# Low half of a weight chunk: one VectorE subtract over 1024 columns in place of two over 512

## The chip, the cores and the metric

One core of a Trainium2 chip. The metric is the device time of one execution in microseconds (us); a change counts by the median of its runs beside runs of the kernel before on the same chip.

## The reference, cut to what matters

The program is a chain of two models on 256 tokens of width 1024: a two-layer block (gated feed-forward, a mixer, feed-forward again, a gated per-layer embedding), then a two-layer block with modulation, pooling, attention and a squared-ReLU feed-forward of width 4096. Nearly all its arithmetic is matrix products with float32 weights.

```python
def swiglu(x, w_in, w_out):
    gate, up = jnp.split(x @ w_in, 2, axis=-1)
    return (jax.nn.silu(gate) * up) @ w_out

def first_block(x, ...):                       # two layers
    h = h + 0.5 * rmsnorm(swiglu(rmsnorm(h, g[0]), ffn1_w_in[i], ffn1_w_out[i]), g[1])
    h = h + rmsnorm(mix, g[3])                  # even_mixer, then odd_mixer
    h = h + 0.5 * rmsnorm(swiglu(rmsnorm(h, g[4]), ffn2_w_in[i], ffn2_w_out[i]), g[5])
    h = h + rmsnorm(jax.nn.sigmoid(h @ ple_w_gate[i]) * (p[i] @ ple_w_proj[i]), g[6])

def second_block(x, c, ctx, ...):              # two layers, latent and context tokens
    h_lat = h_lat + g1[:, None, :] * y_l        # pool_mix, then attn_mix
    h_lat = h_lat + g2[:, None, :] * sq_relu_mlp(m_l, mlp_w1[i], mlp_w2[i])
    return rms_norm(h_lat, final_g)
```

## The kernel before, in words

Weights stream from HBM once, in chunks of 128 partitions by 1024 float32 columns (512 KB). `split` (L221 to L236) takes in one chunk: a DMA on SP's queue (L227) fills a tile `raw`, ScalarE (ACT) rounds it into the high part `wh` (L232), and VectorE (DVE) makes the low part `wl` as `raw - wh` (L235), in two instructions over 512 columns each. `mm3` (L238 to L241) then makes each product out of three matmuls: high times high, and the two products of a high and a low part. Depending on the stage, the weight is the matmul's moving operand (512 columns at a time, `tok_group`, `out_multi`) or its stationary one (128 columns at a time, `feat_tile`, which goes through the eight 128-column blocks of a chunk in order).

Buffers: four `raw` tiles (`NRAW`), seven pairs of `wh` and `wl` (`NR`), so a chunk can be split up to seven chunks ahead of its matmuls. `raw` comes free when both ACT and DVE have read it. A few chunks go through tiles of their own: `rawx`, `whx`, `wlx` at the end of a feed-forward block, `rawf`, `whf`, `wlf` for the context tokens. In all there are 534 chunks.

DVE has other work: the small steps of the junctions between stages (`xTl` L336, `yt` L362, `h` L367, `ta`, `aro`, `mmx`, the low parts of activations L245 and L250), and side work that makes modulation vectors (`jka` L974, 1024 columns each). GpSimd (POOL) makes the reciprocal roots of the norms: DVE writes a mean square (`ms`, L272 or L296), POOL raises it to the power -0.5 (`rs`, L274 or L298), DVE goes on with the product by it (`mxn` L1010 and L1092, `axn` L1315, `h` L367). The tile framework plans the order of the instructions of each engine at build time, by priorities that follow the program's order and by when an instruction can start in its plan; each engine then runs its list in that order. In that plan the two halves of a chunk are two instructions, and other DVE work may stand between them.

Of the kernel before, what the change touches and what calls it, by code (L numbers as in the profile page):

```python
# [9 lines left out]
F32 = mybir.dt.float32  # L10
# [4 lines left out]
ALU = mybir.AluOpType  # L15
# [154 lines left out]
def tile_model(ctx: ExitStack, tc: tile.TileContext, A, out):  # L170
    nc = tc.nc
    V, S, G, T, Y = nc.vector, nc.scalar, nc.gpsimd, nc.tensor, nc.sync
# [24 lines left out]
    for t in range(2):  # L197
        for n in range(2):
            sl = slice(512 * n, 512 * n + 512)
# [21 lines left out]
    def split(r, chunk, i, wp=None):  # L221
        wpool, wt, wb = wp or (r.w, r.tag, None)
        if wp:
            src = wpool.tile([128, 1024], F32, name="raw" + wt, tag="raw" + wt, bufs=RXB)
        else:
            src = r.raw.tile([128, 1024], F32, name="raw" + r.tag, tag="raw" + r.tag)
        Y.dma_start(src, chunk[:, 1024 * i:1024 * i + 1024])  # L227
        wh = wpool.tile([128, 1024], F32R, name="wh" + wt, tag="wh" + wt, bufs=wb)
        wl = wpool.tile([128, 1024], F32R, name="wl" + wt, tag="wl" + wt, bufs=wb)
        cnt[0] += 1  # L230
        with after(fed[0]) if KEEP < cnt[0] <= KEEP + LATE and r is M else nullcontext():
            S.activation(wh, src, AF.Copy)  # L232
            for q in range(2):
                sl = slice(512 * q, 512 * q + 512)
                V.tensor_tensor(wl[:, sl], src[:, sl], wh[:, sl].bitcast(F32), op=ALU.subtract)  # L235
        return wh, wl  # L236

    def mm3(o, a, b, first, last):  # L238
# [109 lines left out]
    def after(ins):  # L348
        return tc.issue_after(ins) if ins is not None else nullcontext()
# [80 lines left out]
    def out_multi(items, acc, first, last, step=None, extra=0, pool=None, tail=False):  # L430
        ws = []
        for q, (c, hid, k0) in enumerate(items):
            wp = (pool, "x", 2 * extra) if q < extra else None
            ws += [(split(M, c, i, wp), hid, k0 + i) for i in range(2)]
        m = len(ws)
        for t in range(2):
            js = [j for j in range(m)]
            if t and tail:
                order = [(sl, j) for sl in TAIL for j in js]
            elif t:  # L440
                js = js[2 * extra:] + js[:2 * extra]
                order = [(n, j) for j in js for n in range(2)]
            else:
                order = [(n, j) for n in range(2) for j in js[:-2]] + [(n, j) for n in range(2) for j in js[-2:]]
            for n, j in order:
                w, hid, k = ws[j]
                sl = n if isinstance(n, slice) else slice(512 * n, 512 * n + 512)
                mm3(acc[t][:, sl], xk(hid, k, t), (w[0][:, sl], w[1][:, sl]), first and j == 0,
                    last and j == js[-1])
            if step is not None:  # L450
                step(t)
# [6 lines left out]
    def ffn(x, win, wout, np_, pool, hooks, joint):  # L458
# [16 lines left out]
        def inp(i):  # L475
            hid = xt_tiles(2, pool, "hid", 4)
            for j in range(2):
                ps = bank(name="fin")
                for u in range(2):
                    feat_tile(ps[:, 256 * u:256 * u + 256], split(M, win[2 * i + j], u), x.xt)  # L480
                s = pool.tile([128, 256], F32, name="sil", tag="sil", bufs=2)
                V.tensor_tensor(s, ps[:, 0:256], rb, op=ALU.mult)
                S.activation(s, s, AF.Silu)
                V.tensor_tensor(s, s, ps[:, 256:512], op=ALU.mult)
                hilo(hid[0][:, j, :], hid[1][:, j, :], s)
            return hid
# [46 lines left out]
    def group512(chunks, xt, skew=False, name="g5"):  # L533
        ps = pacc.tile([128, 1024], F32, name=name, tag="acc")
        ps = ps.rearrange("p (t n) -> p t n", t=2)
        if skew:
            ws = [split(M, c, u) for c in chunks for u in range(2)]
            tok_group(ps, xt, ws, 0, 8, 512, True, True)
        else:
            for i in range(2):  # L540
                tok_group(ps, xt, [split(M, chunks[i], u) for u in range(2)], 4 * i, 4, 512, i == 0, i == 1)
        return ps
# [1070 lines left out]
```

## Time and profile before

| | us |
|---|---|
| median of 3 runs | 1932.61 (1931.67 to 1932.79) |
| span of the profiled execution | 1926.2 |
| busy: PE matmul | 1856.4 |
| busy: DVE | 1338.0 |
| busy: ACT | 925.8 |
| busy: POOL | 56.8 |

The span goes from the first instruction to the last of one profiled execution; the time of a run holds what lies around it too. The profiled execution's own time outside the span is not shown; between its span and the median lie 6.4 us. Busy time of an engine is the time in which at least one of its instructions ran. Matmuls overlap, so PE's busy time says where PE had nothing to do, not how near it is to its peak.

### The profile page before, as it was taken

What the parts mean: (1) busy time and instruction counts of PE and PEld (TensorE: products, weight loads), DVE (VectorE), ACT (ScalarE), POOL (GpSimd) and SP (SyncE); (2) the same over time, 40 slices, a digit from 0 to 9 for tenths busy, and PEclk for the clock granted to TensorE, in tenths of its full rate; (3) what the DMA queues carried; (4) which work ended last, traced back from release to release, by engine and by line L of the source; (5) the groups of instructions that cost most, each with busy time, mean ns of one, the idle gap of its engine ahead of it and who ended that gap; (6) DMA issues with size and microseconds to landing.
All of it is one profiled execution on the core that took longest, in us unless ns stands there. A gap on an engine that the chain in (4) does not pass through costs nothing.

```text
span 1926.2 us, 29706 instructions
## 1 busy us (share of the span) xinstructions
PE 1856.4 (96%) x11425; PEld 1636.7 (85%) x11425; DVE 1338.0 (69%) x2531; ACT 925.8 (48%) x1452; POOL 56.8 (3%) x95
## 2 busy tenths in 40 slices
PE   7999999999989999999999998899999999999998
PEld 6999777899969998888789997798999987667997
DVE  6997666999679976765587867854444468656555
ACT  6544657544474445444454455632323335544443
POOL 0000000000000000000000000100000002000000
PEclk9999999999999999999999999999999999999999
DMA  8886534887568865655488857333232324216552
GB/s 274 286 272 223 173 104 144 278 276 256 161 213 269 276 217 192 230 164 166 159 280 306 300 191 255 130 112 99 88 101 98 98 67 134 88 61 196 191 186 78
DMA packets 100950, 356.06 MB, mean 185 GB/s; under 512 B 12249, under 2 KB 13129, under 8 KB 100809
## 3 DMA queue, kind: packets, MB, share of 16 engines
q1 hardware_dynamic: 100088, 353.30, 55.2%
q8 instruction: 89, 1.46, 0.3%
q10 hardware_dynamic: 720, 0.88, 0.1%
q14 instruction: 53, 0.43, 0.1%
HBM read 353.03 MB, written 1.10 MB: 184 GB/s over the span
## 4 chain that ended last, share of the span: by engine, by line
PE 75%; issue 11%; DVE 6%; ACT 3%; DMA 3%; POOL 2%; SPq 0%; POOLq 0%; ACTq 0%; DVEq 0%
PE finm L239 8%; PE finm L241 8%; PE finm L240 8%; PE acc L239 8%; PE acc L241 7%; PE acc L240 7%; PE g L241 2%; PE g L239 2%; PE g L240 2%; PE mfinm L239 2%; PE mfinm L241 2%; PE mfinm L240 2%; DVE wlm L235 2%; PE cfof L239 2%; PE cfof L241 1%
## 5 line engine op out<-in xcount | busy, mean ns | idle before, releaser
L235 DVE TENSOR_TENSOR wlm<-rawm,whm 128x512 fp32r<-128x512 f32 x1048 | 683.8, 686 | 340.3 <-ACT whm L232 337.3
L232 ACT ACTIVATE whm<-rawm 128x1024 fp32r<-128x1024 f32 x524 | 550.1, 1058 | 560.0 <-PE finm L240 154.8
L239 PE MATMUL finm<-xTh,whm 128*128 128x256 f32 x1280 | 362.6, 283 | 0.0
L240 PE MATMUL finm<-xTl,whm 128*128 128x256 f32 x1280 | 362.5, 283 | 0.0
L241 PE MATMUL finm<-xTh,wlm 128*128 128x256 f32 x1280 | 362.5, 283 | 0.0
L240 PEld LDWEIGHTS finm<-xTl,whm 128*128 128x128 f32 x1280 | 243.7, 190 | 1.7
L239 PEld LDWEIGHTS finm<-xTh,whm 128*128 128x128 f32 x1280 | 243.8, 190 | 1.6
L241 PEld LDWEIGHTS finm<-xTh,wlm 128*128 128x128 f32 x1280 | 243.6, 190 | 0.0
L239 PE MATMUL acc<-whm,hidh 128*128 128x512 f32 x544 | 215.6, 397 | 1.9 <-ACT hidh L244 1.9
L241 PE MATMUL acc<-whm,hidl 128*128 128x512 f32 x544 | 214.8, 395 | 0.0
L240 PE MATMUL acc<-wlm,hidh 128*128 128x512 f32 x544 | 214.4, 395 | 0.0
L974 DVE SCALAR_TENSOR_TENSOR jka<-rawa,sv 128x1024 bf16<-128x1024 f32 x160 | 195.2, 1220 | 27.2 <-DMA rawa<-in_adw_dram 26.4
L239 PE MATMUL g<-whm,xTh 128*128 128x512 f32 x320 | 129.4, 404 | 10.1 <-ACT xTh L335 3.4
L241 PE MATMUL mfinm<-xTh,wlm 128*128 128x256 f32 x480 | 135.7, 283 | 0.0
L240 PE MATMUL mfinm<-xTl,whm 128*128 128x256 f32 x480 | 135.5, 282 | 0.0
L239 PE MATMUL mfinm<-xTh,whm 128*128 128x256 f32 x480 | 135.4, 283 | 0.0
L241 PE MATMUL g<-whm,xTl 128*128 128x512 f32 x320 | 129.2, 404 | 0.5 <-DVE xTl L250 0.4
L240 PE MATMUL g<-wlm,xTh 128*128 128x512 f32 x320 | 127.6, 399 | 0.0
L239 PEld LDWEIGHTS acc<-whm,hidh 128*128 128x128 f32 x544 | 103.4, 190 | 23.6 <-ACT hidh L244 3.4
L241 PEld LDWEIGHTS acc<-whm,hidl 128*128 128x128 f32 x544 | 102.8, 189 | 22.2 <-DVE hidl L245 0.5
L240 PEld LDWEIGHTS acc<-wlm,hidh 128*128 128x128 f32 x544 | 103.0, 189 | 21.3 <-DVE wlm L235 0.2
L239 PEld LDWEIGHTS mfinm<-xTh,whm 128*128 128x128 f32 x480 | 91.4, 190 | 0.7
(465 smaller groups left out, 3130.0 us busy)
## 6 DMA issues: line engine op xcount, KB each, us to landing
rawm<-in_m_dram SPq DMA_DIRECT2D x128, 512.0 KB, 3.7
rawa<-in_adw_dram SPq DMA_DIRECT2D x96, 512.0 KB, 5.5
rawm<-in_f1i_dram SPq DMA_DIRECT2D x88, 512.0 KB, 5.1
rawm<-in_f2i_dram SPq DMA_DIRECT2D x88, 512.0 KB, 4.9
rawm<-in_odi_dram SPq DMA_DIRECT2D x48, 512.0 KB, 4.3
rawm<-in_f1o_dram SPq DMA_DIRECT2D x40, 512.0 KB, 5.8
rawm<-in_f2o_dram SPq DMA_DIRECT2D x40, 512.0 KB, 5.3
rawm<-in_evi_dram SPq DMA_DIRECT2D x22, 512.0 KB, 4.0
```

Of the source, the lines that this page charges most:

```text
L232: S.activation(wh, src, AF.Copy)
L235: V.tensor_tensor(wl[:, sl], src[:, sl], wh[:, sl].bitcast(F32), op=ALU.subtract)
L239: T.matmul(o, a[0], b[0], start=first, stop=False)
L240: T.matmul(o, a[0], b[1], start=False, stop=False)
L241: T.matmul(o, a[1], b[0], start=False, stop=last)
L974: V.scalar_tensor_tensor(jk, src, 1.0, sv[v], op0=ALU.mult, op1=ALU.mult, accum_out=adacol[:, l, v, 2 * i + f:2 * i + f + 1])
```

## The change

The loop over two halves goes; one instruction computes all 1024 columns of `wl`. Nothing else is changed: the same data, tiles, DMAs and matmuls.

```diff
         with after(fed[0]) if KEEP < cnt[0] <= KEEP + LATE and r is M else nullcontext():
             S.activation(wh, src, AF.Copy)
-            for q in range(2):
-                sl = slice(512 * q, 512 * q + 512)
-                V.tensor_tensor(wl[:, sl], src[:, sl], wh[:, sl].bitcast(F32), op=ALU.subtract)
+            V.tensor_tensor(wl, src, wh.bitcast(F32), op=ALU.subtract)
         return wh, wl
```

## Rows read from the trace of the kernel before

**Rows 1.** The page: span, busy time and instructions of each engine.
```profile
span 1926.2 us, 29706 instructions
PE 1856.4 (96%) x11425; PEld 1636.7 (85%) x11425; DVE 1338.0 (69%) x2531; ACT 925.8 (48%) x1452; POOL 56.8 (3%) x95
```
**Rows 2.** Busy time by stretch: length, PE, PEld, DVE, ACT, POOL, granted clock, DMA.
```profile
320.00:352.00 32.00, 26.63 (x120) 20.03 (x120) 25.48 (x55) 24.44 (x46) 3.99 (x8) 0.95 0.71 244
352.00:545.00 193.00, 192.97 (x1305) 178.48 (x1304) 159.60 (x291) 91.50 (x123) 1.12 (x2) 1.00 0.69 233
...
1155.00:1245.00 90.00, 77.58 (x458) 66.30 (x457) 73.68 (x146) 54.01 (x106) 8.58 (x13) 0.94 0.58 198
1245.00:1560.00 315.00, 315.00 (x2077) 287.06 (x2076) 145.54 (x228) 95.55 (x120) 0.00 (x0) 1.00 0.31 99
1560.00:1745.00 185.00, 171.26 (x776) 130.54 (x774) 128.75 (x300) 91.63 (x210) 16.77 (x14) 1.00 0.29 94
```
**Rows 3.** Waits over the span: who waited for whom, us, times, longest.
```profile
DVE wlm L235 <- ACT whm L232: 337.3, 198, 8.2
...
ACT whm L232 <- PE finm L240: 154.8, 102, 4.0
```
**Rows 4.** Lines L235 and L890: instructions of each kind, ns min/median/max, first and last.
```profile
L235 DVE TENSOR_TENSOR wlm<-rawm,whm x1048: 671/685/695, 9.7 to 1899.5; 128x512 fp32r<-128x512 f32 x175
...
L235 DVE TENSOR_TENSOR wlx<-rawx,whx x16: 670/684/686, 51.7 to 977.5; 128x512 fp32r<-128x512 f32 x16
...
L890 DVE TENSOR_TENSOR y<-y,ronb x4: 1217/1226/1227, 793.3 to 910.4; 128x1024 f32<-128x1024 f32 x4
```
**Rows 5.** DVE's timeline at two places: start us, us, what.
```profile
66.23 1.29 DVE L235 TENSOR_TENSOR wlm<-rawm,whm 128x512 fp32r<-128x512 f32 x2
67.44 1.22 DVE L974 SCALAR_TENSOR_TENSOR jka<-rawa,sv 128x1024 bf16<-128x1024 f32 x1
...
793.27 1.22 DVE L890 TENSOR_TENSOR y<-y,ronb 128x1024 f32<-128x1024 f32 x1
794.41 0.41 DVE L897 TENSOR_TENSOR oam<-oattm,decay 128x256 f32<-128x256 f32 x1
```
**Rows 6.** The chain by line: whole span, then 1155 to 1245, 1605 to 1660 us.
```profile
PE finm L239 8%; PE finm L241 8%; PE finm L240 8%; PE acc L239 8%; PE acc L241 7%; PE acc L240 7%; PE g L241 2%; PE g L239 2%; PE g L240 2%; PE mfinm L239 2%; PE mfinm L241 2%; PE mfinm L240 2%; DVE wlm L235 2%; PE cfof L239 2%; PE cfof L241 1%
...
by line: DMA prow<-rows 10.6%; DMA rawf<-in_plw_dram 8.0%; DVE wlm L235 6.7%; issue 5.7%; PE pptf L1051 5.1%; DMA wmt<-in_wm_dram 3.5%; DVE h L367 3.2%; ACT mmx L1022 3.0%; POOL rsf L298 2.7%; DVE yt L1080 2.7%; ACT jkg L343 2.5%; DVE xTl L
...
by line: DVE wlm L235 13.7%; POOL rsm L274 12.0%; issue 5.9%; ACT jkm L268 5.5%; DVE axn L1315 5.1%; ACT whm L232 3.5%; PE atpm L1403 3.1%; PE ckv L241 2.9%; PE ckv L240 2.9%; PE lkv L241 2.8%; PE lkv L240 2.5%; POOL rsf L274 2.5%; PE ckv L
```
**Rows 7.** Who waited for the low halves of L235: us, times, longest.
```profile
  PEld cfof L240: 0.8, 1
  PEld g L240: 0.6, 2
...
  PEld cpmf L240: 0.2, 1
```
**Rows 8.** PE's timeline at the longest of these waits, and DVE's beside it.
```profile
1238.46 0.50 PE L240 MATMUL cfof<-wlm,hich 128*128 128x512 f32 x1 [0.61 <-DVE wlm L235]
...
1234.73 0.68 DVE L235 TENSOR_TENSOR wlm<-rawm,whm 128x512 fp32r<-128x512 f32 x1
...
1237.72 0.68 DVE L235 TENSOR_TENSOR wlm<-rawm,whm 128x512 fp32r<-128x512 f32 x1
```
**Rows 9.** POOL's timeline, powers of line L298.
```profile
1197.05 0.93 POOL L298 TENSOR_TENSOR rsf<-msf,nhalf 128x1 f32<-128x1 f32 x1 [24.08 <-DVE msf L296]
...
1213.36 0.57 POOL L298 TENSOR_TENSOR rsm<-msm,nhalf 128x1 f32<-128x1 f32 x1
...
1734.38 0.94 POOL L298 TENSOR_TENSOR rx<-msx,nhalf 128x1 f32<-128x1 f32 x1 [8.32 <-DVE msx L296]
```
**Rows 10.** DVE's timeline around the first of these powers.
```profile
1196.89 0.68 DVE L235 TENSOR_TENSOR wlm<-rawm,whm 128x512 fp32r<-128x512 f32 x1
1198.02 0.75 DVE L1010 TENSOR_SCALAR mxn<-hc,rsf 128x1024 f32<-128x1024 f32 x1 [0.44 <-POOL rsf L298]
```

## The prediction

> **What bounds the kernel now.** I read four views in this order: the page, the busy times by stretch, the list of waits, and the chain of work that ended last. On the page TensorE has matmuls running for 1856.4 of 1926.2 us; DVE is busy for 1338.0 us [rows 1]. So about 70 us are left in which PE has nothing to do, and a faster DVE can only win there. The stretches show where they lie. In 352 to 545 us PE is busy for 192.97 of 193.00 us though DVE is busy for 159.60, and in 1245 to 1560 us for all of it [rows 2]: in the long stages PE alone sets the time. The rest is at the junctions between stages: 320 to 352 us (5.4 us open), 1155 to 1245 us (12.4 us) and 1560 to 1745 us (13.7 us) [rows 2], then others like them.
>
> The waits say why the weights don't matter in the long stages. DVE waits 337.3 us for ACT's high parts, and ACT in turn waits for PE to give a weight buffer back, 154.8 us behind one group of matmuls alone [rows 3]. The ring of seven buffers is full, and ACT and DVE run ahead of PE. A low half that is ready 0.5 us later or 0.1 us earlier is not seen there. The question is the junctions, where DVE carries the small steps as well.
>
> **The change part by part.** *What one chunk costs on DVE.* A half takes 685 ns at the median; the one row of the same kind over 1024 columns, the product at L890, takes 1226 ns [rows 4]. But instructions overlap at their ends: two halves last 1.29 us together, and the next instruction starts 1.21 us after the first one (66.23 to 67.44). Behind the 1024-column product the next starts after 1.14 us (793.27 to 794.41) [rows 5]. So one chunk frees 0.07 us of DVE's queue and its last column is ready 1.29 - 1.22 = 0.07 us earlier, while its first half is ready 1.22 - 0.69 = 0.53 us later. Over the 532 chunks of [rows 4] (1048 and 16 halves) the queue gains 37 us, nearly all beside a busy PE.
>
> The Trainium skill (VectorE: DVE Perf Modes, section on the DRAIN you can't avoid) says that the next operation doesn't start until the pipe is empty. By that rule two halves would hold DVE for 1.37 us and a chunk would free 0.15 us; the overlap in the rows above disagrees, and term A below would be larger by 19 pairs at 0.08 us, 1.5 us, and the time 1930.1 us.
>
> *Term A, DVE's shorter queue on the path.* In the chain the low halves hold 2% of the span, some 38 us [rows 6]. At 0.605 us a half these are 64 halves or 32 pairs: 32 x 0.07 = 2.2 us at most. Where PE really has holes they hold 6.7% of 90 us and 13.7% of 55 us [rows 6], together 13.6 us, 11 pairs, 0.8 us. I take 1.3 us, nearer to the stretches, since other junctions have a few pairs too. A = -1.3 us, between -2.2 and 0.
>
> *Term B, the first half later.* PE's own waits for low halves are few: cfof 0.8, two at g 0.6, one at cpmf 0.2 us [rows 7]. Those at g lie at the very start of the program, which waits for its first loads in any case. At cpmf the first columns come 0.53 us later. At cfof it is the other way: PE waits from 1237.85 to 1238.46 for the second half of a chunk whose first half was done three microseconds before it [rows 8]; as one instruction at 1234.73 the chunk is whole at 1235.95 and this wait (0.6 us) goes, though what stood behind that half is put off by 0.53 us. Ends -0.6 and +1.1 us; they nearly cancel, and I take +0.2.
>
> *Term C, the halves as fillers.* At the junctions the plan puts one half into the hole that DVE has while POOL makes a reciprocal root. This hole is not free. With nothing beside it the power takes 0.57 us; with a half started just before it, 0.93 and 0.94 us [rows 9]. At 1196.89 us the half runs to 1197.57, the power ends at 1197.98, and DVE's next step starts at 1198.02 [rows 9, 10]: POOL ends 0.41 us behind the half, whatever its own start. If a whole chunk stands there, it ends at 1198.11 and the power 0.41 us later, at 1198.52: 0.53 us more on the way to `mxn`. Seven such powers with a low half beside them stand in the chain, the first and the last of them in [rows 9]: 7 x 0.53 = +3.7 us. The Trainium skill bears on this (GPSIMD Engine Reference, section Specifications: the SBUF interfaces are shared with VectorE, with contention for instructions with two SBUF inputs, as this subtract is); it gives no figure, and the rows agree with it.
>
> Against that stands the other half. A chunk in a hole is a chunk whose second half no longer stands among the small steps. Six of the seven holes lie in the two stretches in which DVE's queue is the chain for long parts (1155 to 1245 and 1605 to 1660 us), and there each half taken out of the queue gives back 0.605 us: 6 x 0.605 = -3.6 us. C is between -3.6 (the holes cost nothing more) and +3.7 us (nothing is taken out); I take the sum, +0.1.
>
> *What follows.* `raw` is released when DVE is done, so 0.07 us earlier; SP issues the next load that much earlier. That is hidden where the ring is full. No wait, DMA or semaphore user is added; SP, ACT and POOL keep their instructions. A longer DVE instruction holds up what is queued behind it by up to 1.14 in place of 0.605 us: `sil`, `xTl` and `h` at the junctions wait for it, and PE's transposes for them; this is the same 0.53 us per place as in C. Not bounded by any row: the plan itself. The order of every engine is planned anew with one instruction in place of two, and neighbours may change places. TensorE's clock: in 320 to 352 us the granted mean is 0.95 [rows 2], which is some 3.2 us at 1.2 GHz after PE had stood still; one more or one less such spell moves at most half of it, 1.6 us.
>
> The sum: -1.3 + 0.2 + 0.1 = -1.0 us. The profiled execution has a span of 1926.2 us and 6.4 us around it up to the median; the change touches the span alone, so 1925.2 + 6.4 = 1931.6 us.
>
> **The rivals.** *Slower: POOL held behind whole chunks.* The seven powers each wait 0.53 us more, and no half leaves the path, because the plan puts the freed place to another chunk; a few POOL steps ahead of a gate's product at the block starts are held up likewise, say four, 2.1 us. 3.7 + 2.1 - 1.3 = +4.5 us: 1937.1 us. It decides when more than about seven of the small chains get a whole chunk in front. For it speaks that the powers end 0.41 us behind a half in the rows; against it that DVE's total in those stretches falls.
>
> *Faster: the holes take whole chunks and the queue is emptied.* C at its lower end and A as taken: -3.6 - 1.3 = -4.9, so 1927.7 us. For it speaks that DVE is idle for 0.44 us even behind a hole that a half has filled [rows 10]; against it that this idle time is POOL's own 0.41 us behind the half, which moves with it.
>
> *It doesn't do what it says.* The subtract over 1024 columns costs as much as two halves, A falls away and B and C stay: +0.3 us, 1932.9. The product at L890, with the same kinds of operands, speaks against it [rows 4].
>
> **How the numbers follow.** No difference of note (the sum as taken, with small changes of order) gets 0.47, the third rival 0.03 within the same band, the slower rival 0.30 and the faster one 0.20. About 0.2%, 3.9 us, is what a measurement of this kernel can tell from no change. So faster 0.20, same 0.50, slower 0.30. The range: the low end is near the faster case, 1927.5; all lower ends together (-2.2 - 0.6 - 3.6) would give 1926.2. The high end takes the slower case and a part of a clock spell, 1938.0; all upper ends together (0 + 1.1 + 3.7 + 1.6) give 1939.0.
>
> **What would show it.** In the profile of the changed kernel the subtract should appear as 534 instructions of about 1.22 us and DVE's busy time fall by some 37 us. The long stretches (352 to 545, 1245 to 1560 us) should keep their length. The powers of L298 with a low part beside them should take some 1.4 to 1.5 us; if they stay at 0.93 us the plan has kept chunks out of the holes, and if they are 1.5 us while PE's open time in 1155 to 1245 and 1605 to 1660 us stays, halves were given back as in C. PE's wait at cfof for a second half should be gone. The prediction is wrong if a long stretch changes its length, or if the plan moves work between stages, which would show as other neighbours on PE's queue.

## The result and the profile after

The changed kernel takes 1951.86 us (median, 1951.01 to 1954.3) beside 1932.14 us for the kernel before on the same chip: 1.0105 times as long, 95% interval 1.0092 to 1.0118. It is slower by about 20 us; the forecast was 1931.6 us, no difference, and the range ended at 1938.0.

The page of the changed kernel first, span and engines [rows 1]:

```profile
span 1952.2 us, 29130 instructions
...
PE 1869.4 (96%) x11425; PEld 1641.4 (84%) x11425; DVE 1305.1 (67%) x1997; ACT 923.7 (47%) x1454; POOL 60.3 (3%) x95
```

DVE has 534 instructions fewer and is busy for 32.9 us less, and nothing of this reaches the end. PE runs the same 11425 matmuls, 13.0 us longer, and stands still for 82.8 in place of 69.8 us. Next the line of the low halves, L233 here (lines behind it are two lower than in [rows 4], where it is L235): duration in ns as min/median/max, and further down who waited for it.

```profile
L233 DVE TENSOR_TENSOR wlm<-rawm,whm x524: 1204/1222/1228, 9.6 to 1925.1; 128x1024 fp32r<-128x1024 f32 x175
...
who waited for it (us, times):
...
  PEld g L238: 1.0, 1
```

1222 ns, as forecast from one row of L890. The wait at `cfof` is gone; PE's other waits for low parts stay small (1.0 us at `g` in place of 0.6, 0.3 at `cpmf` in place of 0.2 [rows 7]). The change does what it says. The stretches that answer to [rows 2] (length, then PE, PEld, DVE, ACT, POOL, granted clock, DMA):

```profile
334.00:366.00 32.00, 25.53 (x91) 17.51 (x92) 25.11 (x48) 19.08 (x37) 3.59 (x7) 0.79 0.63 196
366.00:559.00 193.00, 192.12 (x1299) 177.83 (x1299) 151.43 (x218) 91.21 (x122) 1.12 (x2) 1.00 0.70 226
1268.00:1583.00 315.00, 315.00 (x2071) 286.27 (x2070) 142.15 (x170) 95.81 (x120) 0.00 (x0) 1.00 0.32 98
1583.00:1770.00 187.00, 172.07 (x774) 131.72 (x773) 126.30 (x267) 90.79 (x209) 16.60 (x14) 0.99 0.30 94
```

These windows are laid beside those of [rows 2], the first three of the same length. In the two long stages PE is busy almost without a break, as before; by the start times compared below the second of them grows by 0.9 to 1.2 us. At the junctions it is not: in the first of these rows PE is busy for 1.1 us less than in 320 to 352 us before, and at a mean clock of 0.79 in place of 0.95 [rows 2].

To find where the time goes, the start of the same matmul in two traces is compared. The table has the growth of the delay against the trace of [rows 1], by stretches of that trace. The second column is another execution of the kernel before, whose run took 1932.45 us with a span of 1930.6 us.

| us of the first trace of before | before, again | changed | changed, again |
|---|---|---|---|
| 0 to 251 | -1.6 | -1.3 | -0.1 |
| 251 to 508 | 0.0 | +15.3 | +12.7 |
| 508 to 756 | +0.1 | +1.5 | +0.9 |
| 756 to 831 | +0.4 | +2.9 | +2.5 |
| 831 to 1139 | +5.9 | +5.2 | +5.8 |
| 1139 to 1256 | -0.1 | -0.3 | -1.4 |
| 1256 to 1572 | -0.1 | +0.9 | +1.2 |
| 1572 to the last matmuls | -0.1 | +2.2 | +5.4 |

The second column matters. 831 to 1139 us looked like a loss of 5 us, and the kernel before has it as well in its other execution: it is the first trace that was short there. What belongs to the change is one large site, 13 to 15 us in 251 to 508 us, and small pieces at 508 to 831 us (4.4 and 3.4) and behind 1572 us (2.2 and 5.4).

The large site in rows. It is the end of the second gated recurrence and the junction behind it. ACT, DVE and POOL of the changed kernel at the recurrence's last steps (start us, us, what):

```profile
315.78 0.28 ACT L266 ACTIVATE jkm<-ohgm 128x128 bf16<-128x128 f32 x1 [3.17 <-PE ohgm L815]
...
316.21 1.06 ACT L232 ACTIVATE whm<-rawm 128x1024 fp32r<-128x1024 f32 x1
...
317.82 1.05 ACT L232 ACTIVATE whm<-rawm 128x1024 fp32r<-128x1024 f32 x1
318.78 0.26 ACT L266 ACTIVATE jkm<-ohgm 128x128 bf16<-128x128 f32 x1
```
```profile
320.05 0.16 DVE L270 TENSOR_SCALAR msm<-hssm 128x4 f32<-128x4 f32 x1
320.12 1.22 DVE L233 TENSOR_TENSOR wlm<-rawm,whm 128x1024 fp32r<-128x1024 f32 x1
322.25 1.13 DVE L821 SCALAR_TENSOR_TENSOR sg<-ohgm,rsm,sg 128x128 f32<-128x128 f32 x4 [0.91 <-POOL rsm L272]
```
```profile
320.29 1.92 POOL L272 TENSOR_TENSOR rsm<-msm,nhalf 128x4 f32<-128x4 f32 x1 [71.26 <-DVE msm L270]
```

And the same steps in the kernel before:

```profile
313.00 0.28 ACT L268 ACTIVATE jkm<-ohgm 128x128 bf16<-128x128 f32 x1 [0.84 <-PE ohgm L817]
...
314.20 0.28 ACT L268 ACTIVATE jkm<-ohgm 128x128 bf16<-128x128 f32 x1
...
314.61 1.06 ACT L232 ACTIVATE whm<-rawm 128x1024 fp32r<-128x1024 f32 x1
```
```profile
314.85 1.01 POOL L274 TENSOR_TENSOR rsm<-msm,nhalf 128x4 f32<-128x4 f32 x1 [64.47 <-DVE msm L272]
```
```profile
315.90 1.13 DVE L823 SCALAR_TENSOR_TENSOR sg<-ohgm,rsm,sg 128x128 f32<-128x128 f32 x4 [1.13 <-POOL rsm L274]
```

Before, ACT's four sums of squares stand together (313.00 to 314.20) and the product `sg` starts 2.90 us after the first of them (315.90). Now the first sum waits 3.17 us for PE's products `ohgm` (0.84 before), two copies `whm` of 1.06 us lie between the sums, a whole chunk lies beside POOL's power, which takes 1.92 in place of 1.01 us, and `sg` starts 6.47 us after the first sum. PE waits 2.49 us for it (0.81 before):

```profile
322.74 1.01 PE L825 MATMUL oatm<-identt,sg 128*128 128x128 f32 x4 [2.49 <-DVE sg L821]
```

Then the junction. ACT's queue has the SILU of the side work (L977) ahead of copies that PE's next product needs, and this SILU waits for its load:

```profile
347.21 1.06 ACT L977 ACTIVATE sv<-sv 128x1024 f32<-128x1024 f32 x1 [3.96 <-DMA sv<-in_cc_dram]
348.17 0.61 ACT L333 ACTIVATE xTh<-tpsm,gct 128x128 fp32r<-128x128 f32 x2
```
```profile
348.57 0.79 PE L237 MATMUL g<-whm,xTh 128*128 128x512 f32 x1 [3.11 <-ACT xTh L333]
```

None of these neighbours stood so in the kernel before. Only DVE's instructions were changed, but 275 lines of PE's order differ between the two built programs. The traces show it too: compared as lists, 175 of PE's 11425 matmuls, 76 of ACT's 1452 instructions and 52 of SP's 698 transfers stand elsewhere.

### The profile page after: what moved, and what is told of

Its sections match the earlier page's. It is cut to its first block, busy times and chain, and to the rows that moved or that the text cites. A ratio compares the mean times of both kernels' runs of the same rounds, so it can differ in the third digit from the quotient of the medians.

```text
span 1952.2 us, 29130 instructions
## 1 busy us (share of the span) xinstructions
PE 1869.4 (96%) x11425; PEld 1641.4 (84%) x11425; DVE 1305.1 (67%) x1997; ACT 923.7 (47%) x1454; POOL 60.3 (3%) x95
## 3 DMA queue, kind: packets, MB, share of 16 engines
q8 instruction: 89, 1.46, 0.3%
## 5 line engine op out<-in xcount | busy, mean ns | idle before, releaser
L233 DVE TENSOR_TENSOR wlm<-rawm,whm 128x1024 fp32r<-128x1024 f32 x524 | 635.6, 1221 | 347.6 <-ACT whm L232 343.3
```

What stands on the lines that cost most here:

```text
L233: V.tensor_tensor(wl, src, wh.bitcast(F32), op=ALU.subtract)
```

## The experiments

Two ideas were set against each other. Theory P: the loss comes from the order that the framework planned anew for all engines. Rival G: the longer instruction itself costs it, since small steps and POOL's powers are held up behind whole chunks. The measured times are given as ratios to the kernel before, run beside each kernel on the same chip, with 95% intervals; "us more" is the ratio's excess times 1932 us. A program is planned twice in the order experiments: once as one kernel, to read off each engine's order; then the other kernel's instructions are tied to that order, engine by engine, with edges that only fix the order of issue and add no wait. The edits are given in outline.

**Order and instruction apart.**

```diff
+    plan = order(build(halves))             # e2: order(build(whole)), per engine
     with tile.TileContext(nc) as tc:
         tile_model(tc, aps, out)             # e1: whole chunks; e2: halves
+        for row in plan.values():
+            for a, b in zip(row, row[1:]):   # b stands behind a on its engine
+                tc.add_manual_dep(b, a, NoSync)
```

> The whole-chunk subtract of the changed kernel, but every engine's instructions stand in the order that the kernel before has (each whole subtract at the place of its first half). Theory P, the loss of 20 us comes from the order that was planned anew and not from the longer instruction: 1929 to 1936 us, within 0.2% of the kernel before. Rival G, the longer instruction itself costs the time (a first half 0.53 us later, small steps and powers held behind whole chunks): 1946 to 1954 us, as the changed kernel's 1951.9.

> Two subtracts over 512 columns for each chunk, as in the kernel before, but every engine's instructions stand in the order of the changed kernel (the second half straight behind the first). Theory P (order): 1947 to 1956 us though no instruction is longer than before; with the 0.07 us per chunk that the halves cost DVE more, rather at the upper end. Rival G (longer instruction): 1929 to 1937 us.

Measured: 1.0051 (1.0035 to 1.0067), 9.8 us more, and 1.0153 (1.0134 to 1.0171), 29.6 us more. Neither idea gives both numbers. In the traces PE, ACT and SP run exactly the lists of the kernel before in e1, and those of the changed kernel in e2. With no instruction longer than before, the new order costs 29.6 us, so G can't be the whole; and whole chunks in the old order still cost 9.8 us, so P can't be either. By stretches the two are clean: in 251 to 508 us e1 loses 0.5 us and e2 12.9, as the changed kernel does. The large site is the order. e1 loses its time elsewhere, 7.9 us in 1256 to 1572 us, a long stage in which PE is busy without a break in the kernel before.

**A whole chunk in front of a small step.** DVE's timeline in that stage, the kernel before and then e1:

```profile
1295.67 0.69 DVE L235 TENSOR_TENSOR wlm<-rawm,whm 128x512 fp32r<-128x512 f32 x1 [1.06 <-ACT whm L232]
1296.28 0.68 DVE L1034 TENSOR_TENSOR rl<-rl 128x512 f32<-128x512 f32 x1
1296.88 1.28 DVE L1206 TENSOR_TENSOR ac<-ac,cfof 128x512 f32<-128x512 f32 x2
1298.08 0.68 DVE L245 TENSOR_TENSOR hidl<-rl,hidh 128x512 fp32r<-128x512 f32 x1
1298.68 0.68 DVE L235 TENSOR_TENSOR wlm<-rawm,whm 128x512 fp32r<-128x512 f32 x1
```
```profile
1299.87 1.23 DVE L235 TENSOR_TENSOR wlm<-rawm,whm 128x1024 fp32r<-128x1024 f32 x1 [1.06 <-ACT whm L232]
1301.01 0.68 DVE L1034 TENSOR_TENSOR rl<-rl 128x512 f32<-128x512 f32 x1
1301.62 1.28 DVE L1206 TENSOR_TENSOR ac<-ac,cfof 128x512 f32<-128x512 f32 x2
```

`ac` (L1206) adds a context product to its sum and so gives PE its PSUM bank back. Before, it starts 1.21 us after the first half, and in e1 1.75 us after the chunk: the 0.54 us that a whole chunk lasts longer. Who waited for `ac`, before and in e1:

```profile
who waited for it (us, times):
  PEld cfof L239: 2.3, 13
```
```profile
who waited for it (us, times):
  PEld cfof L239: 9.3, 13
  PE cfof L239: 3.7, 13
```

Thirteen times PE's weight load, and now PE, stands behind `ac`. In the trace of the kernel before, the two halves of 186 of the 534 chunks have other DVE work between them; that is what a whole chunk takes away. Two kernels move the whole chunk to its second half's place, one everywhere, one in that stage alone:

```diff
-        second halves leave the plan's row                  # e1: chunk stands at its first half's place
+        first halves leave it, the chunk at its second      # e5: all chunks; e11: those of 1255 to 1571 us
```

> As the whole chunks in the order of before, but each whole subtract stands at the place of its second half in place of the first. Theory Q, what the whole chunk costs in that order is the 0.6 us by which it holds up the small steps that stood between the halves (ac in the context products, sil and its gate in the last feed-forward block, 8 and 2.9 us in the trace): at the second half's place they go ahead of it, and the time is 1929 to 1935 us. Rival R, the late first half costs as much (PE waits for low parts): 1938 to 1945 us.

> Whole chunks in the order of before, each at its first half's place, but in the long stage with the context products (1255 to 1571 us) at its second half's place, behind the sum ac that frees PE's bank. Theory Q, the 0.63 us per context chunk that the first of these kernels lost there are the sum ac held up behind a whole chunk: 8.0 us of its 9.8 go, 1931 to 1935 us. Rival R, the late first half takes its place in that stage: 1938 to 1943 us.

e11 takes 1.0015 (1.0006 to 1.0024), 2.9 us more, and its trace loses 1.0 us in 1256 to 1572 us in place of 7.9: theory Q holds for that stage. e5 takes 1.0069 (1.0058 to 1.0081), 13.3 us more, and its median of 1946.75 us is above both bands: it loses nothing in that stage (-0.3 us), but 5.7 us in 1139 to 1256 us, where PE waits 4.0 us for the low parts of the first context products (0.6 before), and 3.5 us more than e1 in the first 251 us (where two executions of one kernel differ by up to 1.6 us). So both are right, each at its place: where a small step follows, the early chunk costs; where PE waits for the weight, the late one does. Two halves can do both.

**Halves parted in the new order.** e2's halves stood straight behind each other. Here they are free to part:

```diff
-        second halves tied behind their first halves   # e2
+        second halves not tied; the plan places them   # e12
```

> Two halves for each chunk; PE, ACT, SP, POOL and DVE's other work in the order of the changed kernel, but the second halves stand where the plan finds room for them (246 of the 534 chunks have other work between their halves; in the earlier run with halves in this order none had). Theory Q, it is the undivided chunk that costs about 10 us, whether it is one instruction or two: 1948 to 1953 us, some 10 us less than the 1961 of that run. Rival, halves only make DVE's queue longer: 1957 to 1963 us.

1.0097 (1.0079 to 1.0114), 18.7 us more, some 11 us less than e2, as theory Q had it. And 18.7 us stay though the instructions are those of the kernel before and the halves are parted: that is the order's. But theory Q's "one instruction or two" does not hold in this order, for the changed kernel has undivided chunks as well and is at 20.3 us. All six cases in us more than the kernel before (e10 is told further down; it also has products in three of PE's holes):

| | halves parted | halves straight behind each other | one instruction |
|---|---|---|---|
| order of before | 0 | 12.2 (e10) | 9.8 (e1) |
| order of the changed kernel | 18.7 (e12) | 29.6 (e2) | 20.3 |

The two costs do not add. In the order of before the long instruction costs 9.8 us against parted halves; in the new order 1.6 us, which the intervals do not tell from nothing. And between e2 and the changed kernel only the number of DVE's instructions differs: one in place of two is some 9 us faster there, spread over the stages.

The stage with `ac` shows how the new order avoids e1's 7.9 us. On DVE the changed kernel has the same order as e1, and `ac` starts as late behind the chunk, 1.75 us:

```profile
1318.99 1.23 DVE L233 TENSOR_TENSOR wlm<-rawm,whm 128x1024 fp32r<-128x1024 f32 x1 [1.06 <-ACT whm L232]
...
1320.74 1.28 DVE L1204 TENSOR_TENSOR ac<-ac,cfof 128x512 f32<-128x512 f32 x2
```

PE's order is what differs. Between the two groups of `cfof` products that need the bank, e1 has two products `acc`, as the kernel before, and then waits; the changed kernel has four, and does not wait. The last of them and the `cfof` behind, e1 first:

```profile
1301.67 0.40 PE L240 MATMUL acc<-wlm,hidh 128*128 128x512 f32 x1
1302.35 0.51 PE L239 MATMUL cfof<-whm,hich 128*128 128x512 f32 x1 [0.28 <-DVE ac L1206]
```
```profile
1321.02 0.39 PE L239 MATMUL acc<-whm,hidl 128*128 128x512 f32 x1
1321.25 0.39 PE L237 MATMUL acc<-whm,hidh 128*128 128x512 f32 x1
1321.48 0.49 PE L237 MATMUL cfof<-whm,hich 128*128 128x512 f32 x1
```

It is so at all 13 places. The plan made for the long instruction hides its price here; what it loses, it loses at the junctions.

**The large site alone.** The order of before in one stretch, on all engines (e3) or on ACT alone (e8), and one edge for the side work's SILU (e4):

```diff
-        for row in plan.values():
+        for row in part(plan, first="hgrn(1)", last="ffn first()"):   # e8: ACT's row only
```
```diff
-        S.activation(tile_, tile_, AF.Silu)
+        with tc.issue_after(last_xTh_copy):        # e4
+            S.activation(tile_, tile_, AF.Silu)
```

> The changed kernel with the order of before in one stretch alone: from the second gated recurrence's own steps to the first product of the next feed-forward block (290 to 351 us in the profile of before); the rest is planned as the framework wants. Theory P with one main site: this stretch is where the two traces part by 14 to 15 us, so 1935 to 1941 us. Rival: the loss is spread or comes back at other places (a later site waits for what this one no longer delays): 1946 to 1953 us.

> The changed kernel with the order of before on ACT alone, in the one stretch from the second gated recurrence's steps to the next feed-forward block's first product; PE, DVE and SP are planned around it. Theory A, ACT's order (weight copies between the four sums of squares, the side work's SILU ahead of the copies for PE) carries the site: its 13.4 us shrink to 0 to 4, 1938 to 1944 us. Rival B, PE's own order carries it (the products that covered the recurrence's end stand before it): 1947 to 1953 us.

> The changed kernel with one edge of order more: in the feed-forward block after the first mixer, ACT's SILU of the side work (which waits 3.96 us for its load, with the copies for PE's next product queued behind it) stands behind the last of these copies. Theory S, that this wait is a part of the loss: 4 us and up to 2 us of TensorE at its lower clock behind the hole go, 1945.5 to 1948.5 us. Rival: the hole is filled by the next late thing (the low parts from DVE, or a weight chunk): 1950 to 1953 us.

e3: 1.0053 (1.0034 to 1.0073), 10.2 us more, so half of the 20.3 us goes with the order of this one stretch. Its trace shows the site gone (1.5 us in 251 to 508 us); 2.0 and 2.3 us in 508 to 756 and 756 to 831 us stay, and 3.8 us behind 1572 us. Its median, 1942.95 us, is a little above the band that was expected; the site is worth 10 us by the times, less than the 13 to 15 us of single traces.

e8: 1.0082 (1.0068 to 1.0096), 15.8 us more, between the two theories. Its trace says why: from 307 to 346 us of the first trace, where the sums and the SILU lie, it loses 0.6 us in place of the changed kernel's 12.1; but at 307 us, where ACT's old order has met a PE order made anew, it is already 4.9 us behind the first trace of before, the changed kernel 1.3. So in this trace ACT's order carries the part with the rows above, and the mixed order loses time ahead of it.

e4: 1.0096 (1.0074 to 1.0117), not to be told from the changed kernel. The delay at 346 us is 5.0 us smaller in its trace, but it has lost 5.3 us behind 1572 us in that execution, as the changed kernel did in its second one (5.4). What the SILU alone is worth stays open.

**Other plans.** Two more ways to cut a chunk, each planned anew:

```diff
-            for q in range(2):
+            for q, e in ((0, 256), (256, 512), (512, 768), (768, 1024)):   # e6; e7: (0, 448), (448, 1024)
```

> Four subtracts over 256 columns for each chunk, planned anew; PE's order differs from before in 214 lines (that of the changed kernel in 275). Theory P, a plan made anew loses time whatever the grain: 1938 to 1955 us. Rival G, only a longer instruction loses: finer fillers cost nothing beyond DVE's own queue (some 0.15 us per chunk more, nearly all beside PE), 1930 to 1936 us.

> Two subtracts for each chunk, over 448 and 576 columns, planned anew; DVE's work is that of before, PE's order differs from before in 102 lines. Theory P: a plan that differs less loses less, 1932 to 1942 us. Rival G (grain alone): 1930 to 1934 us, no measurable difference.

e6: 1.0077 (1.0063 to 1.0091), 14.9 us more; e7: 1.0029 (1.0019 to 1.0039), 5.6 us more. Both go with theory P: finer pieces lose, too, and two pieces of nearly the old size, with the same number of instructions, lose 5.6 us. The more lines of PE's order differ in the built programs (102, 214, 275), the more is lost (5.6, 14.9, 20.3 us); three points are no law, and e6 has also more instructions on DVE.

**Second traces.** Both kernels unchanged, once more.

> The kernel before once more, for a second trace of it. Theory: the long stages and the stretch 290 to 351 us stand where they stood, within 1 us, and what is steady there may be compared between single traces. Rival: 973 to 1139 us, where the small steps of the last feed-forward block meet the side work's loads, is longer by 3 to 6 us in another execution, and the 3 to 5 us that the traces of the changed kernels lost there are no effect of the chunk.

> The changed kernel once more: 1949 to 1955 us, and its main site (290 to 351 us) again 13 to 15 us longer than before's; the smaller sites (545 to 597, 768 to 808, 973 to 1139 us) again 2 to 3, 3 and 5 us if they belong to its order, and other values if they belong to the single execution.

The kernel before: 1932.45 us. The changed one: 1.0109 (1.0081 to 1.0136). The table above holds both. PE's waits in 974 to 1144 us of the second execution of before (who waited for whom, us, times, longest) tell the first two columns apart:

```profile
PE tpsm L416 <- DVE sil L468: 3.5, 1, 3.5
PE finm L239 <- DVE sil L484: 3.0, 3, 1.6
```

The first line is in the first trace as well, the second is not: `sil` (L484) was late three times in one execution and never in the other, at the place where DVE's queue waits for the side work's loads.

**The clock behind the holes.** After each of the two long holes of PE at the large site the granted clock falls to 1.2 GHz; this looked like a second price. PE was given products of constants in the holes:

```diff
+                for _ in range(n):        # a bank that nothing reads, or that the next instruction overwrites
+                    T.matmul(ps[:, 0:256], ones, C["axl"], start=True, stop=True)
```

> The changed kernel with its own order, and PE given work that is of no use to the result in two holes of the main site: five products of constants ahead of the transposes at oatm, six ahead of the product g after the mixer (about 0.47 us each, less than the 2.49 and 3.11 us that PE stands still there). Theory C, that the clock makes the holes dearer: TensorE shows 1.2 GHz in 323 to 330 and 347 to 357 us behind them, 3.7 and 5.3 us of full clock lost; with the holes filled these spells go and the time is 1943 to 1947 us. Rival W, the stretch is bound by the waiting and not by PE's speed: 1950 to 1954 us.

> The changed kernel in its own order with five products of constants ahead of oatm and six in the middle of the product g, at the place where PE waits 3.11 us for xTh (in the earlier run they stood at its start, before the hole). Theory C, the clock doubles what the two holes cost: both spells at 1.2 GHz go and with them 6 to 9 us, 1943 to 1947 us. Rival W, the waiting and not PE's speed sets the end of this stretch: 1950 to 1955 us.

> The changed kernel in its own order with five products of constants ahead of oatm and five in the hole itself, ahead of the product g's second step for the second 128 tokens (the two earlier tries stood beside that hole, and the second one's products ran at 1.2 GHz for 4.6 us). Theory C: the spell at 1.2 GHz behind each hole goes and with both 5 to 8 us, 1944 to 1948 us. Rival W, the waiting and not PE's speed sets the end: 1950 to 1954 us.

> The kernel before with its own order, and six such products ahead of the first transposes of sil in three feed-forward blocks, where PE stands still for 3.2, 3.3 and 3.5 us and then shows 1.2 GHz in 346 to 350, 574 to 582 and 977 to 982 us (1.7, 3.5 and 2.1 us of full clock lost). Theory C: these 7.3 us go in part or whole, 1925 to 1929 us, faster than both kernels. Rival W: 1931 to 1936 us.

> The kernel before with its own order, halves parted as it has them (the earlier run with filled holes had them straight behind each other, which its expectation did not say), and six products of constants in each of the three holes ahead of sil's transposes. Theory C, by the 1.0 us that each hole gave in that run: 1928 to 1931 us. Rival W, no gain: 1931.5 to 1935 us.

Only e17 and e13 are what they were meant to be. In e9 the second group of products stood at the start of the product `g`, ahead of the hole, and in e14 behind it, where the products took 4.8 us, most of it at 1.2 GHz; they gave 1.0121 (1.0106 to 1.0136) and 1.0131 (1.0115 to 1.0146). In e10 the halves stood straight behind each other, not in the order of before as its expectation says: 1.0063 (1.0049 to 1.0077), and its trace loses 0.6 to 0.7 us per context chunk, just as e1's does. That miss is a useful one: in the order of before, two instructions of the old size, never parted, cost about what the one long instruction costs. In the new order they cost more (e2 against the changed kernel).

e17 has the products in both holes. The granted clock (last but two in a row) of the changed kernel's second execution, then of e17:

```profile
322.00:332.00 10.00, 7.25 (x25) 5.58 (x26) 3.58 (x7) 2.47 (x6) 1.44 (x1) 0.83 0.81 279
348.00:358.00 10.00, 8.59 (x21) 5.42 (x21) 8.16 (x17) 7.54 (x15) 3.03 (x6) 0.66 0.49 159
358.00:368.00 10.00, 9.07 (x54) 8.11 (x55) 7.84 (x13) 3.14 (x6) 0.00 (x0) 0.83 0.76 223
```
```profile
322.00:332.00 10.00, 9.01 (x39) 6.87 (x38) 4.94 (x9) 3.69 (x7) 1.92 (x1) 1.00 0.83 268
348.00:358.00 10.00, 7.35 (x21) 4.55 (x21) 7.42 (x16) 7.68 (x15) 3.03 (x6) 0.83 0.44 141
358.00:368.00 10.00, 8.54 (x62) 7.65 (x63) 9.12 (x14) 3.22 (x6) 0.00 (x0) 1.00 0.74 237
```

The clock is back but for one spell (351.5 to 354.9 us in e17's trace), and the time is not: 1.0110 (1.0094 to 1.0125) beside 1.0109 of the changed kernel on the same chip. The 5 to 8 us of theory C are not there. A smaller gain is not ruled out: e17's trace grows by 10.4 us in 251 to 508 us in place of 12.7 and 15.3, and it is longer at other places. On the kernel before (e13), products in the three holes ahead of `sil` give 0.9986 (0.9974 to 0.9997), 2.7 us less: a small gain, the only version faster than both kernels, and it owes nothing to the change. e13 and e17 are also tied to their own kernel's order throughout, so the edges themselves cost nothing that shows.

## Why the prediction was wrong

*What bounds the kernel* held for the two kernels: the long stages kept their length within about 1 us and the loss is at the junctions. But "a low half that is ready 0.5 us later is not seen there" was read too widely. It is true of the low half and not of the small steps behind it: in the order of before, whole chunks cost 7.9 us in a stage where PE was busy for all of 315.00 us [rows 2], through `ac`. PE without idle time said that `ac` was early enough, not by how much. The changed kernel escapes there because its PE order has two products more ahead of the one that needs `ac`.

*What one chunk costs on DVE* was right: 1222 ns, and 32.9 us less of DVE's busy time (forecast 37). The rule of the Trainium skill that was weighed against it (VectorE: DVE Perf Modes, section on the DRAIN you can't avoid: an operation starts when the pipe is empty) would have made it 0.15 us a chunk, some 80 us by that estimate. The same section adds that an operation that is not held starts earlier, and with that the trace agrees: 0.06 us a chunk.

*Term A* (-1.3 us) is not seen against parted halves: e11, which has the whole gain on DVE and the old order, is 2.9 us slower than before, not faster. Only against two halves straight behind each other does the shorter work show, by some 9 us in the new order (e2 and the changed kernel).

*Term B*: PE's wait at `cfof` is gone, as forecast [rows 7, 8]. Its other waits changed by 0.5 us or less in the changed kernel's two traces, but for one of 1.4 us in the second (at `pptf`). Its upper side showed only in e5, 5.7 us where chunks stand late.

*Term C* had its mechanism right. The powers over one column (the lines of [rows 9]) take 1.46 and 1.47 us with a whole chunk beside them, as forecast. Four of the forecast's seven are over four columns (L274, here L272), which take 1.01 us with nothing beside them. In the changed kernel:

```profile
1227.16 1.46 POOL L296 TENSOR_TENSOR rsm<-msm,nhalf 128x1 f32<-128x1 f32 x1 [1.00 <-DVE msm L294]
...
1635.71 1.92 POOL L272 TENSOR_TENSOR rsf<-msf,nhalf 128x4 f32<-128x4 f32 x1 [8.02 <-DVE msf L270]
1641.22 1.01 POOL L272 TENSOR_TENSOR rsm<-msm,nhalf 128x4 f32<-128x4 f32 x1 [3.59 <-DVE msm L270]
...
1759.37 1.47 POOL L296 TENSOR_TENSOR rx<-msx,nhalf 128x1 f32<-128x1 f32 x1 [8.33 <-DVE msx L294]
```

Of the seven, four now have a whole chunk beside them, and three have none (as at 1641.22): a chunk in one hole leaves the next one empty, which is the giving back that C counted on. Together the seven powers take 9.7 in place of 8.7 us. Three other powers have got a chunk, the one at the large site among them. What all this makes in time can't be told apart from the new order: 1139 to 1256 us is not longer (-0.3 and -1.4 us), behind 1572 us 2.2 and 5.4 us are lost. It was not what decided.

*The step that failed* is the sentence "Not bounded by any row: the plan itself". The unknown was seen and then given no term, no width and no rival; the text's own sign of failure, other neighbours on PE's queue, is what came: 275 lines of PE's order. With the instructions of before, parted, this new order costs 18.7 of the 20.3 us (e12), and one stretch of it 10 us (e3). The slower rival had a chance of 0.30 but the wrong price: it counted POOL's powers at 0.53 us each, 4.5 us in all, where a change of order moved whole groups of steps. The order could have been had without a time, by laying the two programs' orders side by side; what the 275 lines cost could not, but the range would have been wider.

The clock term (1.6 us at most) was too small as a description: a mean of 0.79 in 334 to 366 us is 6.7 us of full clock lost, against 1.6 us in 320 to 352 us before. But with these spells mostly gone e17 takes the same time, so at most a few of the 20 us lie there.

*The sum's base* was misread. The 6.4 us between span and median are not around the span: the changed kernel's profiled execution took 1954.3 us with a span of 1952.2, so 2.1 us lie around it, and the execution of [rows 1] was a short one, by 4.4 us against the second trace. It changes nothing in the forecast, since the difference was added back, but it made 831 to 1139 us look like a loss.

What stays open: why the framework's plan is worse for undivided chunks, and how the 10 us outside the large site divide among the other junctions; they differ by up to 3 us between two executions of the same kernel (2.2 and 5.4 us behind 1572 us). Open is also how much of the large site is PE's slower clock.

## What to carry to other kernels

Where a framework plans the order of all engines, an edit to one instruction is also an edit to every queue: compare the two orders engine by engine, and if they differ, time the new instruction in the old order and the old instruction in the new order before explaining anything. Two short instructions are worth more than one long one where the plan puts other work between them: count how often it does (186 of 534 here), and ask which step stands behind the long one, even in a stage where the bound engine never idles. The costs of an instruction and of an order need not add: a plan made for the long instruction can hide it at one place (20.3 us in all, not 9.8 + 18.7). And take a second trace of the kernel before: a site of 5 us here was only the first trace's luck.

## What the runs showed of the hardware

POOL's power over four columns takes 1.01 us with nothing beside it on DVE and 1.92 us with a whole chunk's subtract started 0.17 us ahead of it (320.12 and 320.29); the one over one column takes 0.55 to 0.57 us alone and 1.46 us with a whole chunk. It ends a fixed time behind DVE's instruction: over four columns 0.87 us behind it (at 322.21, the chunk at 321.34), over one column 0.41 us (at 1228.62, the chunk at 1228.21), and the same 0.41 us behind a half chunk [rows 9, 10]. So the forecast from half chunks carried over to whole ones.

The two holes of PE at the large site are followed by several us at 1.2 GHz: in the changed kernel's first execution 323 to 330 us behind the 2.49 us at `oatm` and 347 to 357 us behind the 3.11 us at `g`, in its second execution 3.4 and 6.8 us behind holes of 2.5 and 2.9 us. Products of constants in the holes took most of this away (the mean clock in 322 to 332 us went from 0.83 to 1.00) and did not shorten the kernel (1.0110 beside 1.0109).
